# Splitting MLA queries and keys where the projections write them, and masking the score maxima on VectorE

## The chip, the cores and the metric

The kernel runs on one core of one Trainium2 chip. Its engines work side by side, each through its own queue in order: TensorE (PE in the profile, with its weight loads as PEld), VectorE (DVE), ScalarE (ACT), GpSimd (POOL) and SyncE (SP), which here issues most of the DMA transfers. The metric is the time of one execution on the device in microseconds, lower is better; the kernel before takes 2153.65 us, the median of three executions.

## What is computed

A decoder trunk of two layers over 1024 positions of width 1024. Layer 0 mixes positions by multi-head latent attention (MLA), layer 1 by a sliding window; each has four heads that look at a memory, an output projection and an MLP with squared ReLU. The change touches layer 0's MLA only. In the reference, cut to what matters:

```python
def mla_mixer(hn, positions, w_in, q_norm_g, kv_norm_g, w_uq, w_ukv):
    b, s, _ = hn.shape
    proj = hn @ w_in
    c_q, c_kv, k_r, q_cross = ...            # 384, 256, 32 and 256 columns
    q = (rmsnorm(c_q, q_norm_g) @ w_uq).reshape(b, s, 12, 96)
    q = jnp.concatenate([q[..., :64], rope(q[..., 64:], positions)], axis=-1)
    kv = (rmsnorm(c_kv, kv_norm_g) @ w_ukv).reshape(b, s, 12, 128)
    k_nope, v = kv[..., :64], kv[..., 64:]
    k_rope = jnp.broadcast_to(rope(k_r[:, :, None, :], positions), (b, s, 12, 32))
    k = jnp.concatenate([k_nope, k_rope], axis=-1)
    o = causal_dense_attention(q, k, v)      # softmax of q k / sqrt(96), k at or before q
    return o.reshape(b, s, 768), q_cross
```

There are 12 heads; a query or key has 64 columns of its own (nope) and 32 rotated ones (rope), and the rotated key is the same for all heads.

## The kernel before

A product in the kernel's precision is three matmuls. An operand `a` is split into a head `ah`, rounded to the TensorE format fp32r, and a rest `al = a - ah` (`split`, L96: ScalarE copies and rounds, L99; VectorE subtracts, L100; with a scale the same on L102 and L103). The matmuls are `ah bh`, `ah bl` and `al bh` (`mm3`, L108 to L110).

**Projection stage** (182 to 245 us of the span). `cTh` and `cTl` hold the split latent input, transposed. For each pair j of heads (6 of them) the nope keys come from TensorE into a PSUM tile `pskn` of 1024 positions and are copied whole in f32 to `kn[j]`, half by VectorE (L765) and half by ScalarE (L766). Then the rotary queries, eight position tiles t of 128: `q_rope(t)` multiplies (`psqr`) and rotates (`rope`, four VectorE products L302 to L305, two GpSimd sums L306 and L307, into a row tile `qt` in the quad tile `fa`); `q_ropeT(t)` transposes it on TensorE (`psqt`, L793) and ScalarE copies it to `qr` (L794, L795; two thirds of it lie in the tile `kq`). Between them `load_cols` brings the weights of the nope queries, nine pieces `wr` through two buffers (L533), and splits them into `wqn` and `wqn2`. `q_nope(j, i)` then makes the nope queries of pair j, half i of the positions (`psqn`), and copies them to `qn[j]` by ScalarE (i = 0, L777) or VectorE (L775).

**Head tiles.** `head_tiles(h)` collects the 96 rows of one head into staging tiles `q32` and `k32` by four DMAs (L710 to L713), and splits them into `qh`, `ql`, `kh`, `kl` (12 heads, tiles of 96 x 1024, in three sets `bufs_`). Row 96 of these tiles holds a row of ones (in the keys, L703) and the row's maximum (in the queries, L732 and L733), so that the scores come out with the maximum taken off. Set 0 has its own place; sets 1 and 2 lie in a pool `hb1` that takes the place of `cTh` and the weights after the projection stage.

**Head loop** (245 to 472 us). For head h the program runs `row_max` ahead: for each of eight query tiles i the scores of all keys up to the tile (`psx`, one matmul of heads only per 512 columns, L743), then a matmul of an identity with a mask that adds -1e30 above the diagonal (L744), then VectorE's maximum (L745). Rows with i > 3 use the one PSUM buffer "x", of two banks; those with i up to 3 share six buffers of one bank with all else. `max_row` transposes and splits the maxima. Then come the score blocks `scores(h, G, k)` (`pss`, three matmuls L865; a mask add on VectorE for diagonal blocks, L873; exponent on ScalarE, L875) and `values` (`pso`, L895). The score blocks of one head, its values and the maxima of a later head are interleaved. The values of head h are split by `v_tiles(h)` for all eight key tiles (`vh`, `vl`); key tiles 0 to 3 of the first half of the queries use the split, all blocks of the second half use unsplit values `vf`.

The order on each engine is that of the program after a scheduler has placed it; DMA issues stand in SP's queue in order, and one that waits holds those behind it.

Of the kernel before, what the change touches and what calls it, by code (L numbers as in the profile page):

```python
# [19 lines left out]
P = 128  # L20
D = 1024
S = 1024
# [33 lines left out]
def trunk(  # L56
# [450 lines left out]
    masks(pm)  # L507
# [197 lines left out]

    def head_tiles(h):
        r = slice((h % 2) * 64, (h % 2) * 64 + 64)
        q32 = hb.tile([96, S], F32, tag="q32", bufs=1, name=f"q32_{h}")
        k32 = hb.tile([96, S], F32, tag="k32", bufs=1, name=f"k32_{h}")
        nc.sync.dma_start(out=q32[0:64], in_=qn[h // 2][r, :])  # L710
        nc.sync.dma_start(out=q32[64:96], in_=qr[h // 4][(h % 4) * 32 : (h % 4) * 32 + 32, :])
        nc.sync.dma_start(out=k32[0:64], in_=kn[h // 2][r, :])
        nc.sync.dma_start(out=k32[64:96], in_=krs)  # L713
# [21 lines left out]
    def row_max(h, i):  # L735
# [5 lines left out]
        for a in range(0, n, 512):  # L741
            b = min(a + 512, n)
            nc.tensor.matmul(ps[:, a:b], qh[0:96, i * P : (i + 1) * P], kh[0:96, a:b], start=True, stop=b < n, skip_group_check=True)  # L743
        nc.tensor.matmul(ps[:, n - P : n], identb, dmask, start=False, stop=True, skip_group_check=True)  # L744
# [7 lines left out]
    krs = raw_tile([32, S], "krs")  # L752
# [3 lines left out]
    nc.vector.tensor_copy(krs, krT)  # L756
    for j in range(6):
# [7 lines left out]
        nc.vector.tensor_copy(kn[j][:, 0:512], ps[:, 0:512])  # L765
        nc.scalar.activation(kn[j][:, 512:1024], ps[:, 512:1024], AF.Copy)  # L766
# [1271 lines left out]
```

## Time and profile before

| | us |
|---|---|
| three executions | 2151.32, 2153.65, 2155.61 |
| median | 2153.65 |
| the profiled execution, time | 2155.25 |
| its span | 2153.2 |
| projection stage, 182 to 245 | 63 |
| head loop, 245 to 472 | 227 |

The span runs from the first to the last instruction on the chip; what lies around it is launch and end. All rows that the prediction quotes are of this one profiled execution. In a timeline row the first number is the start, the second the duration, both in us, then engine, line and operation, output and inputs by the program's names, shapes, and in brackets how long the engine stood idle before it and what released it. In a group row the last parts are the number of instructions, their busy time in us with the mean of one in ns, and the idle time ahead of them.

### The profile page before, as it was taken

Reading aid. Unit: us, or ns where it says so; the run is one execution under the profiler, and the core shown is the slowest. Engines: PE = TensorE matmul, PEld = TensorE weight load, DVE = VectorE, ACT = ScalarE, POOL = GpSimd, SP = SyncE. Lnnn points to the kernel's source line nnn. Section 1 sums busy time; section 2 is a strip of 40 time slices with the busy share of each in tenths; the row PEclk is TensorE's granted clock in tenths of the full one; section 3 lists DMA queues with packets and bytes.
Section 4 is the critical chain, followed back from the end, with each engine's and each line's share of the span. In section 5 each row is a group of like instructions: output and inputs, shape, how many; then the busy total and the mean of one; then the engine's idle time right before and its main releaser. Section 6 shows DMA issues by size and latency. Waiting matters only on the chain.

```text
span 2153.2 us, 29008 instructions
## 1 busy us (share of the span) xinstructions
PE 2121.7 (99%) x9877; PEld 1703.6 (79%) x9877; DVE 1468.2 (68%) x2905; ACT 1100.4 (51%) x2398; POOL 135.1 (6%) x223
## 2 busy tenths in 40 slices
PE   7999999999999999999999999999999999999998
PEld 6988766668887788888888878668888888888886
DVE  7566677764987677786657632775987776876565
ACT  5554465655754444444445432866754443444453
POOL 0001000000000000000001122530000000000000
PEclk9999999999999999999999999999999999999999
DMA  7102221333254445964543534142354446954442
GB/s 251 58 1 75 52 63 39 97 104 108 87 182 133 162 154 178 330 188 135 156 117 108 147 88 119 34 130 83 100 182 144 134 160 200 332 166 150 124 118 88
DMA packets 178498, 284.00 MB, mean 132 GB/s; under 512 B 17209, under 2 KB 73262, under 8 KB 178350
## 3 DMA queue, kind: packets, MB, share of 16 engines
q1 hardware_dynamic: 171908, 266.39, 40.0%
q0 software_dynamic: 4016, 13.12, 1.7%
q10 hardware_dynamic: 2426, 2.65, 0.4%
q8 instruction: 77, 1.26, 0.3%
q14 instruction: 71, 0.58, 0.1%
HBM read 180.13 MB, written 76.81 MB: 119 GB/s over the span
## 4 chain that ended last, share of the span: by engine, by line
PE 88%; DVE 5%; DMA 3%; ACT 2%; issue 1%; SPq 0%; POOL 0%; DVEq 0%; ACTq 0%
PE psy L1665 5%; PE psy L1667 5%; PE psy L1666 5%; PE psu L1362 5%; PE psu L1364 5%; PE psu L1363 5%; PE psz L1665 4%; PE psz L1666 4%; PE psz L1667 4%; PE psv L1362 4%; PE pso L895 4%; PE psv L1363 4%; PE psv L1364 4%; PE pss L865 3%; PE pswo L108 2%; PE pswo L109 2%
## 5 line engine op out<-in xcount | busy, mean ns | idle before, releaser
L1262 ACT ACTIVATE mr<-mr,gcol 128x256 f32<-128x256 f32 (+1 forms) x160 | 67.7, 480 | 79.2 <-DMA mr<-in_mlp_w_up_dram 75.4
L875 ACT ACTIVATE p<-pss 128x512 f32<-128x512 f32 (+2 forms) x144 | 68.6, 487 | 71.9 <-DVE pss L873 53.8
L1665 PE MATMUL psy<-g 128*128 128x512 f32 x256 | 99.9, 390 | 0.0
L1666 PE MATMUL psy<-g 128*128 128x512 f32 x256 | 99.6, 389 | 0.0
L1667 PE MATMUL psy<-g 128*128 128x512 f32 x256 | 99.4, 390 | 0.0
L99 ACT ACTIVATE g<-i 128x512 fp32r<-128x512 f32 x79 | 49.8, 631 | 92.8 <-PE psz L1666 45.9
L1262 ACT ACTIVATE d<-d,gcol 128x256 f32<-128x256 f32 x128 | 57.9, 503 | 71.2 <-DMA d<-in_mlp_w_up_dram 67.8
L100 DVE TENSOR_TENSOR g<-i,g 128x512 fp32r<-128x512 f32 x79 | 55.4, 701 | 48.9 <-ACT g L99 48.9
L99 ACT ACTIVATE i<-mr 128x512 fp32r<-128x512 f32 x78 | 49.3, 632 | 74.5 <-PE psy L1666 24.5
L745 DVE TENSOR_REDUCE m<-psx 128x1 f32<-128x768 f32 (+7 forms) x96 | 71.7, 752 | 22.1 <-PE psx L744 22.0
L99 ACT ACTIVATE uh<-i 128x512 fp32r<-128x512 f32 x66 | 41.8, 633 | 86.5 <-PE psy L1666 39.7
L895 PE MATMUL pso<-p,vf 128*128 128x512 f32 (+2 forms) x192 | 85.3, 528 | 0.0
L100 DVE TENSOR_TENSOR uh<-i,uh 128x512 fp32r<-128x512 f32 x66 | 45.6, 690 | 48.4 <-ACT uh L99 48.4
L1665 PE MATMUL psz<-g 128*128 128x512 f32 x192 | 74.7, 389 | 0.0
L1666 PE MATMUL psz<-g 128*128 128x512 f32 x192 | 74.7, 389 | 0.0
L1667 PE MATMUL psz<-g 128*128 128x512 f32 x192 | 74.7, 389 | 0.0
L100 DVE TENSOR_TENSOR i<-mr,i 128x512 fp32r<-128x512 f32 x78 | 53.6, 687 | 21.8 <-ACT i L99 21.8
L865 PE MATMUL pss<-qh,kh 97*128 97x512 f32 (+2 forms) x144 | 66.1, 464 | 0.1
L865 PE MATMUL pss<-ql,kh 97*128 97x512 f32 (+2 forms) x144 | 57.6, 400 | 0.0
L1578 DVE TENSOR_TENSOR mqf<-mqq,mqf 128x512 f32<-128x512 f32 x64 | 43.4, 688 | 19.3 <-DMA mqq<-in_mlp_w_down_dram 19.1
L1667 PEld LDWEIGHTS psy<-g 128*128 128x128 f32 x256 | 48.0, 188 | 10.0
L1665 PEld LDWEIGHTS psy<-g 128*128 128x128 f32 x256 | 48.1, 188 | 9.9
(645 smaller groups left out, 6861.6 us busy)
## 6 DMA issues: line engine op xcount, KB each, us to landing
i<-hd SPq DMA_DIRECT2D x154, 256.0 KB
hd<-uh SPq DMA_DIRECT2D x76, 256.0 KB
hd<-ul SPq DMA_DIRECT2D x76, 256.0 KB
mr<-in_mlp_w_up_dram SPq DMA_DIRECT2D x36, 512.0 KB
hd<-x SPq DMA_DIRECT2D x72, 256.0 KB
mr<-hd SPq DMA_DIRECT2D x70, 256.0 KB
d<-in_mlp_w_up_dram SPq DMA_DIRECT2D x32, 512.0 KB
mqq<-in_mlp_w_down_dram SPq DMA_DIRECT2D x32, 512.0 KB
```

What stands on the lines that cost most here:

```text
L99: nc.scalar.activation(hi, src, AF.Copy)
L100: nc.vector.tensor_tensor(lo, src, f32(hi), ALU.subtract)
L745: nc.vector.reduce_max(m8s[h][:, i : i + 1], ps[:, :n], axis=AX, negate=True)
L865: return lambda: nc.tensor.matmul(o, a, b, skip_group_check=True, **kw)
L895: mms.append(lambda: nc.tensor.matmul(o, a, b, skip_group_check=True, **kw))
L1262: nc.scalar.activation(w[:, k, :], w[:, k, :], AF.Copy, scale=g_mlp[layer][:, k0 + k : k0 + k + 1])
L1362: nc.tensor.matmul(ps, wh[:, k, :], xh[:, k, :], start=p in (1, 2, 5) and k == 0, stop=False, skip_group_check=True)
L1363: nc.tensor.matmul(ps, wh[:, k, :], xl[:, k, :], start=False, stop=False, skip_group_check=True)
L1364: nc.tensor.matmul(ps, wl[:, k, :], xh[:, k, :], start=False, stop=k == 3, skip_group_check=True)
L1665: nc.tensor.matmul(ps, ah[:, j, :], bh, start=p in (1, 5, 2) and k == 0, stop=False, skip_group_check=True)
L1666: nc.tensor.matmul(ps, ah[:, j, :], bl, start=False, stop=False, skip_group_check=True)
L1667: nc.tensor.matmul(ps, al[:, j, :], bh, start=False, stop=k == NP - 1, skip_group_check=True)
```

## The change

The nope keys, the nope queries, the rotary queries and the rotary key are split as they leave PSUM. The heads go, rounded, to where the f32 values went; the rests go to tiles `lo` (they use the buffers of `q32` and `k32`, in turn) and from there to DRAM tiles `kl_d`, `ql_d` (6 x 512 KB each) and `qrl_d` (8 x 192 KB, from the row tile that the rotation used). The rotary key's rest sits beside its head in `krs`. `head_tiles` now issues eight DMAs that write `qh`, `kh`, `ql`, `kl` directly, and splits nothing. The mask of the maxima's rows is added by VectorE to PSUM ahead of the maximum; the row i = 4, of 640 columns, is written as 320 + 320 around a bank's edge. The splits of the values for key tiles 4 to 7, which no matmul reads, go. `q_nope(0, 0)` stands one place earlier, ahead of the transpose of tile 6. The masks are made by GpSimd alone.

```diff
-    identb, dmask = [const.tile([P, P], BF16, name=n) for n in ("identb", "dmask")]
-    dmaskT = const.tile([P, P], F32, name="dmaskT")
-
-    def masks(pl):
-
-        nc.vector.tensor_copy(identb, ident)
-        for dst, sgn in ((dmask, 1), (dmaskT, -1)):
-            m = pl.tile([P, P], F32, tag="mask", bufs=2, name=f"mask{sgn}")
+    dmask, dmaskT = [const.tile([P, P], F32, name=n) for n in ("dmask", "dmaskT")]
+
+    def masks():
+
+        for m, sgn in ((dmask, 1), (dmaskT, -1)):
             nc.gpsimd.memset(m, 0.0)
             nc.gpsimd.affine_select(out=m, in_=m, compare_op=ALU.is_ge, fill=NEG, base=0, pattern=[[-sgn, P]], channel_multiplier=sgn)
-            nc.vector.tensor_copy(dst, m)
...
+    kl_d, ql_d = [[dram.tile([P, S], F32, name=f"{n}ld{j}") for j in range(6)] for n in "kq"]
+    qrl_d = dram.tile([P, 3, S], F32, name="qrld")
+
     def head_tiles(h):
         r = slice((h % 2) * 64, (h % 2) * 64 + 64)
-        q32 = hb.tile([96, S], F32, tag="q32", bufs=1, name=f"q32_{h}")
-        k32 = hb.tile([96, S], F32, tag="k32", bufs=1, name=f"k32_{h}")
-        nc.sync.dma_start(out=q32[0:64], in_=qn[h // 2][r, :])
-        nc.sync.dma_start(out=q32[64:96], in_=qr[h // 4][(h % 4) * 32 : (h % 4) * 32 + 32, :])
-        nc.sync.dma_start(out=k32[0:64], in_=kn[h // 2][r, :])
-        nc.sync.dma_start(out=k32[64:96], in_=krs)
-        qh, ql, kh, kl = bufs_[h % 3]
+        rr = slice((h % 4) * 32, (h % 4) * 32 + 32)
+        qh, ql, kh, kl = [f32(t_) for t_ in bufs_[h % 3]]
         if h in (1, 2):
             head_ones(h)
-        split(q32, qh[0:96], ql[0:96])
-        split(k32, kh[0:96], kl[0:96])
+        for dst, src in (
+            (qh[0:64], qn[h // 2][r, :]), (qh[64:96], qr[h // 4][rr, :]),
+            (kh[0:64], kn[h // 2][r, :]), (kh[64:96], krs[0:32]),
+            (ql[0:64], ql_d[h // 2][r, :]), (ql[64:96], qrl_d[rr, h // 4, :]),
+            (kl[0:64], kl_d[h // 2][r, :]), (kl[64:96], krs[32:64]),
+        ):
+            nc.sync.dma_start(out=dst, in_=src)
+
+    lo_ct = [0]
+
+    def lo_tile():
+        lo_ct[0] += 1
+        return hb.tile([P, S], F32R, tag=("q32", "k32")[lo_ct[0] % 2], bufs=1, name=f"lo{lo_ct[0]}")
+
+    def fr(ap):
+        return ap.bitcast(F32R)
...
@@ -738,10 +746,13 @@
         qh, ql, kh, kl = bufs_[h % 3]
         n = (i + 1) * P
         ps = psx(f"psx{h}_{i}") if i > 3 or len(psum) == 1 else ps1(f"psx{h}_{i}")
-        for a in range(0, n, 512):
-            b = min(a + 512, n)
-            nc.tensor.matmul(ps[:, a:b], qh[0:96, i * P : (i + 1) * P], kh[0:96, a:b], start=True, stop=b < n, skip_group_check=True)
-        nc.tensor.matmul(ps[:, n - P : n], identb, dmask, start=False, stop=True, skip_group_check=True)
+        if i == 4:
+            ps = ps[:, 192:832]
+        cut = 320 if i == 4 else 512
+        for a in range(0, n, cut):
+            b = min(a + cut, n)
+            nc.tensor.matmul(ps[:, a:b], qh[0:96, i * P : (i + 1) * P], kh[0:96, a:b], start=True, stop=True, skip_group_check=True)
+        nc.vector.tensor_tensor(ps[:, n - P : n], ps[:, n - P : n], dmask, ALU.add)
         nc.vector.reduce_max(m8s[h][:, i : i + 1], ps[:, :n], axis=AX, negate=True)
...
     qr = [kq[1][:, 2, :], kq[1][:, 3, :], raw_tile([P, S], "qr2")]
-    krs = raw_tile([32, S], "krs")
+    krs = raw_tile([64, S], "krs")
-    nc.vector.tensor_copy(krs, krT)
+    split(krT, fr(krs[0:32]), fr(krs[32:64]))
...
@@ -762,8 +773,10 @@
         ps = ps2(f"pskn{j}")
         mm3w([ps[:, s] for s in halves],
              [(wkn[kt][0][:, j * P : (j + 1) * P], wkn[kt][1][:, j * P : (j + 1) * P], [(cTh[:, 3 + kt, s], cTl[:, 3 + kt, s]) for s in halves]) for kt in range(2)])
-        nc.vector.tensor_copy(kn[j][:, 0:512], ps[:, 0:512])
-        nc.scalar.activation(kn[j][:, 512:1024], ps[:, 512:1024], AF.Copy)
+        lo = lo_tile()
+        for s in halves:
+            split(ps[:, s], fr(kn[j][:, s]), lo[:, s])
+        nc.sync.dma_start(out=kl_d[j], in_=f32(lo))
...
     def q_nope(j, i):
         ps = ps1(f"psqn{j}_{i}")
         mm3(ps, [(wqn[kt][0][:, j * P : (j + 1) * P], wqn[kt][1][:, j * P : (j + 1) * P], cTh[:, kt, halves[i]], cTl[:, kt, halves[i]]) for kt in range(3)])
+        if i == 0:
+            qlo[j] = lo_tile()
+        split(ps, fr(qn[j][:, halves[i]]), qlo[j][:, halves[i]])
         if i:
-            nc.vector.tensor_copy(qn[j][:, halves[i]], ps)
-        else:
-            nc.scalar.activation(qn[j][:, halves[i]], ps, AF.Copy)
-
-    qts = {}
+            nc.sync.dma_start(out=ql_d[j], in_=f32(qlo.pop(j)))
+
+    qts, qlo = {}, {}
...
@@ -791,8 +805,12 @@
         pt = ps1(f"psqt{t}")[:, 0:384]
         for i in range(3):
             nc.tensor.transpose(pt[:, i * P : (i + 1) * P], qt[:, i * P : (i + 1) * P], ident)
-        nc.scalar.activation(kq[1][:, 2:4, sl], pt[:, 0 : 2 * P].rearrange("p (k c) -> p k c", k=2), AF.Copy)
-        nc.scalar.activation(qr[2][:, sl], pt[:, 2 * P : 3 * P], AF.Copy)
+
+        lo = fr(qt).rearrange("p (k c) -> p k c", k=3)
+        p3 = pt.rearrange("p (k c) -> p k c", k=3)
+        split(p3[:, 0:2, :], fr(kq[1][:, 2:4, sl]), lo[:, 0:2, :])
+        split(p3[:, 2, :], fr(qr[2][:, sl]), lo[:, 2, :])
+        nc.sync.dma_start(out=qrl_d[:, :, sl], in_=f32(lo))
 
     for t in range(NT):
         q_rope(t)
@@ -800,8 +818,8 @@
             next(loading, None)
         if t > 1:
             q_ropeT(t - 2)
+    q_nope(0, 0)
     q_ropeT(NT - 2)
-    q_nope(0, 0)
     q_nope(0, 1)
     q_ropeT(NT - 1)
...
     for i in range(2):
-        vb = (at.tile([P, NT, 128], F32R, name=f"vh{i}"), at.tile([P, NT, 64], F32R, name=f"vl{i}"))
...
     def v_tiles(h):
         vh, vl = vbufs[h % 2]
-        src = v[:, :, h * 64 : (h + 1) * 64]
```

Three places show what moves. The first is SP's queue in the rotary part of the projection stage; `wr` is a piece of the query weights, the last figures of its name its place among nine. Before:

```order
L533 DMA wr_0_1_1_2109<-in_mla_w_uq_dram 128x384
L533 DMA wr_0_1_2_2137<-in_mla_w_uq_dram 128x384
L533 DMA wr_0_2_0_2165<-in_mla_w_uq_dram 128x384
L533 DMA wr_0_2_1_2193<-in_mla_w_uq_dram 128x384
L533 DMA wr_0_2_2_2221<-in_mla_w_uq_dram 128x384
L711 DMA q_0_2289<-kq_1891 32x1024
```

After (`qrld` is the DRAM tile of rotary rests, `fa` the tile it is stored from):

```order
L529 DMA wr_0_1_1_2141<-in_mla_w_uq_dram 128x384
L529 DMA wr_0_1_2_2172<-in_mla_w_uq_dram 128x384
L813 DMA qrld<-fa_98 384x1x128
L529 DMA wr_0_2_0_2203<-in_mla_w_uq_dram 128x384
L813 DMA qrld<-fa_98 384x1x128
L529 DMA wr_0_2_1_2234<-in_mla_w_uq_dram 128x384
L813 DMA qrld<-fa_98 384x1x128
L529 DMA wr_0_2_2_2265<-in_mla_w_uq_dram 128x384
L813 DMA qrld<-fa_98 384x1x128 x3
```

Between the weight loads now stand stores that each wait for a split; the order of the loads is as before.

The second is SP's queue at the end of the projection stage, where head 1's tiles (`kh_2466`, `kl_2467` before, `qh_2542` to `kl_2545` after) come into use. Before:

```order
L710 DMA q_1_2491<-qn_1889 64x1024
L711 DMA q_1_2491<-kq_1891 32x1024
L732 DMA qh_1897<-mhl_2404 1x8x128
L733 DMA ql_1898<-mhl_2404 1x8x128
L703 DMA kh_2466<-kh_1899 1x16x64
L703 DMA kl_2467<-kl_1900 1x16x64
L710 DMA q_2_2565<-qn_1889 64x1024
```

After (`qld_1894` is the last of the six DRAM tiles of query rests, `lo_2515` what it is stored from):

```order
L791 DMA qld_1893<-lo_2489 128x1024
L699 DMA kh_2544<-kh_1906 1x16x64
L791 DMA qld_1894<-lo_2515 128x1024
L699 DMA kl_2545<-kl_1907 1x16x64
L717 DMA qh_2542<-qn_1896 64x1024
L717 DMA qh_2542<-kq_1898 32x1024
L717 DMA kh_2544<-kq_1897 64x1024
L717 DMA kh_2544<-krs 32x1024
L717 DMA ql_2543<-qld_1889 64x1024
L717 DMA ql_2543<-qrld 32x1024
L717 DMA kl_2545<-kld_1883 64x1024
```

Head 1's loads, which stood ahead of the maxima of head 0 and went to staging tiles, now stand behind the ones rows of its own tiles, with the last store of query rests between them.

The third is TensorE's queue just after the projection stage: score blocks of head 0 (`pss`) and maxima's rows of head 1 (`psx`). Before:

```order
L865 MATMUL pss_1_4_2520<-qh_1897,kh_1899 128x512
L865 MATMUL pss_1_4_2520<-ql_1898,kh_1899 128x512
L865 MATMUL pss_1_4_2520<-qh_1897,kl_1900 128x512
L743 MATMUL psx_7_2528<-kh_2466,qh_2464 128x512 x2
L744 LDWEIGHTS identb
L744 MATMUL psx_7_2528<-dmask,identb 128x128
L865 MATMUL pss_0_1_2533<-qh_1897,kh_1899 128x384
L865 MATMUL pss_0_1_2533<-ql_1898,kh_1899 128x384
L865 MATMUL pss_0_1_2533<-qh_1897,kl_1900 128x384
```

After:

```order
L883 MATMUL pss_1_4_2596<-qh_1904,kh_1906 128x512
L883 MATMUL pss_1_4_2596<-ql_1905,kh_1906 128x512
L883 MATMUL pss_1_4_2596<-qh_1904,kl_1907 128x512
L883 MATMUL pss_0_1_2609<-qh_1904,kh_1906 128x384
L883 MATMUL pss_0_1_2609<-ql_1905,kh_1906 128x384
L883 MATMUL pss_0_1_2609<-qh_1904,kl_1907 128x384
L754 MATMUL psx_7_2604<-kh_2544,qh_2542 128x512 x2
L754 MATMUL psx_3_2621<-kh_2544,qh_2542 128x512
```

The mask matmul and the load of its identity are gone, and the first row of head 1 (`psx_7`) stands one score block later than before.

More of the change, by code (lines that the diff above doesn't have):

```diff
@@ L506, in trunk @@
     rope_tables(pm)
-    masks(pm)
+    masks()
     kv_d = [dram.tile([P, n], F32, name=f"kvd{i}") for i, n in enumerate((1024, 1024, 512))]
@@ L826, in trunk @@
     for i in range(2):
-        vb = (at.tile([P, NT, 128], F32R, name=f"vh{i}"), at.tile([P, NT, 64], F32R, name=f"vl{i}"))
+        vb = (at.tile([P, 4, 128], F32R, name=f"vh{i}"), at.tile([P, 4, 64], F32R, name=f"vl{i}"))
         vbufs.append(vb)
@@ L834, in v_tiles @@
         vh, vl = vbufs[h % 2]
-        src = v[:, :, h * 64 : (h + 1) * 64]
+        src = v[:, 0:4, h * 64 : (h + 1) * 64]
         if h < 2:
```

## The prediction

> **What bounds the kernel now.** I read the engine totals first, then busy time by stage in the windows view, then the timeline of the stages that the diff touches. The first row is the page's; the others give for each stretch its length and what each engine worked in it, the granted clock and the share of the DMA engines.
>
> ```profile
> PE 2121.7 (99%) x9877; PEld 1703.6 (79%) x9877; DVE 1468.2 (68%) x2905; ACT 1100.4 (51%) x2398; POOL 135.1 (6%) x223
> ...
> 182.00:197.60 15.60, 15.60 (x71) 12.88 (x70) 7.20 (x14) 6.64 (x14) 0.00 (x0) 1.00 0.49 145
> 197.60:212.10 14.50, 14.50 (x91) 14.26 (x89) 12.31 (x35) 5.89 (x16) 8.15 (x13) 1.00 0.40 109
> 212.10:221.00 8.90, 6.63 (x27) 5.21 (x25) 2.33 (x8) 2.93 (x9) 1.92 (x3) 0.81 0.00 1
> 221.00:245.00 24.00, 24.00 (x114) 18.85 (x113) 10.47 (x15) 4.93 (x10) 0.65 (x2) 1.00 0.15 34
> 245.00:262.80 17.80, 16.61 (x84) 11.63 (x83) 17.07 (x31) 11.88 (x23) 1.28 (x3) 1.00 0.35 82
> 297.70:315.20 17.50, 17.50 (x87) 12.29 (x87) 12.74 (x25) 11.25 (x23) 0.00 (x0) 1.00 0.28 61
> ```
>
> TensorE is busy 99% of the span, and all of 297.70 to 315.20, one period of the attention's head loop (17.5 us), where VectorE works 12.74 us. So a head gets shorter only by what leaves TensorE, and anything given to VectorE there is free while its answer is not waited for. Of the stretches shown it idles in two: 212.10 to 221.00 (2.27 us, before the query projection's second half) and 245.00 to 262.80 (1.19 us, heads 0 and 1 just after it, where VectorE works 17.07 of 17.80). The change touches both.
>
> **Masks leave TensorE.** 96 mask matmuls go. The rows are the group of those matmuls, VectorE's mask add of the score blocks, and score-maximum rows in the timeline.
>
> ```profile
> L744 PE MATMUL psx<-dmask,identb 128*128 128x128 bf16 x96 | 22.2, 231 | 0.0
> L873 DVE TENSOR_TENSOR pss<-pss,dmaskT 128x128 f32<-128x128 f32 x96 | 27.6, 292 | 14.1 <-PE pss L865 13.5
> ...
> 328.36 0.68 PE L743 MATMUL psx<-kh,qh 96*128 96x512 f32 x2
> 328.89 0.23 PE L744 MATMUL psx<-dmask,identb 128*128 128x128 bf16 x1
> 328.93 0.31 PE L865 MATMUL pss<-qh,kh 97*128 97x128 f32 x1
> 329.16 1.23 DVE L745 TENSOR_REDUCE m<-psx 128x1 f32<-128x1024 f32 x1 [0.29 <-PE psx L744]
> 329.71 0.39 PE L865 MATMUL pss<-qh,kh 97*128 97x512 f32 x1
> 329.94 0.40 PE L865 MATMUL pss<-ql,kh 97*128 97x512 f32 x1
> 330.18 0.40 PE L865 MATMUL pss<-qh,kl 97*128 97x512 f32 x1
> 330.43 0.30 PEld L743 LDWEIGHTS psx<-kh,qh 96*128 96x128 f32 x2 [0.30 <-DVE m L745]
> 331.22 1.09 DVE L745 TENSOR_REDUCE m<-psx 128x1 f32<-128x896 f32 x1 [0.43 <-PE psx L744]
> 333.48 0.51 PE L743 MATMUL psx<-kh,qh 96*128 96x512 f32 x2
> ```
>
> A row's 231 ns is not its price, since matmuls overlap. Starts are: 512 columns come every 0.235 us (329.71, 329.94, 330.18). From 328.36 to 328.93 two of them and the mask take 0.57 us, so the mask takes 0.57 - 0.47 = 0.10 here. Read from the mask's start alone (328.89 to 328.93) it would be 0.04; that is the lower bound, 96 x 0.04 = 3.8 us, and 0.231 x 96 = 22.2 us the upper. I take 0.12, the subtraction and a little for the weights that the mask loads between, since the stage is made of such spacings: **-11.5 us**. The Trainium skill, "TensorE: Matmul & The Clock Gate", section "Back-to-back issue gap", gives a sustained 81 ns for a 128-column matmul with its weight load; by it the term would be 7.8 us, and the sum 3.7 us worse. The one place quoted, 0.10, lies between the two.
>
> In exchange VectorE does 96 adds like L873's (0.292 us). They lie ahead of the reduce on the same PSUM slot, and the rows of over 512 columns have one slot. The row at 330.43 is that cost: the weights of the next such row wait for the reduce until 330.43, while TensorE's spacing (330.18 to 330.43) shows no loss yet: no slack. Afterwards the work between is 0.12 shorter and the reduce ends about 0.29 - 0.12 = 0.17 later, so this one row of a head gives its 0.12 back and pays 0.17: 0.30 us. The next row of the slot has slack: its reduce ends at 331.22 + 1.09 = 332.31, and the one after starts at 333.48, 1.2 us later. It and its like pay nothing. Seven heads of the steady loop have it: 2.1 us; heads 1 and 2, where VectorE is fuller, I set at 0.7. Bounds are 0 (VectorE, relieved below, answers earlier) and 96 x 0.30 = 29 us (every row waits). Taken, by the row with no slack: **+2.8 us**.
>
> **Splits leave the head loop.** Per head two ScalarE copies and two VectorE subtractions go, and half of one values split on each.
>
> ```profile
> L100 DVE TENSOR_TENSOR ql<-q,qh 96x1024 fp32r<-96x1024 f32 x12 | 14.6, 1216 | 3.5 <-ACT qh L99 3.5
> L100 DVE TENSOR_TENSOR kl<-k,kh 96x1024 fp32r<-96x1024 f32 x12 | 14.6, 1214 | 0.4 <-ACT kh L99 0.3
> ...
> 257.23 0.56 PE L743 MATMUL psx<-kh,qh 96*128 96x512 f32 x2 [0.43 <-DVE m L745]
> 259.48 0.33 PE L743 MATMUL psx<-kh,qh 96*128 96x128 f32 x1 [0.43 <-ACT p L875]
> ```
>
> VectorE loses 1.22 + 1.21 = 2.43 us and gains 8 x 0.29 = 2.3 us a head: nothing on balance, so it does not become the bound. But lumps of 1.2 us become pieces of 0.3, and waits like the two of 0.43 us in head 1 are such lumps. I credit those two and about 0.6 us more, **-1.5 us** (0 to -3). In steady heads the eight loads of a head, 1.57 MB in place of 0.79, are issued a head ahead and are needed some 9 us later; at the 262 GB/s of the slice quoted below they take 6 us. Hidden, on a cover of 3 us.
>
> **Head 1 now waits for its loads.** Its four tiles lie where the projection's input lay, which is free only after the last projection matmul at 244.75. Before, the loads went into staging tiles far earlier, and only the splits had to wait for that point. Now the loads themselves do.
>
> ```profile
> 222.23 0.58 SPq L710 DMA_DIRECT2D q<-qn  x1
> 225.25 1.06 ACT L99 ACTIVATE qh<-q 96x1024 fp32r<-96x1024 f32 x1 [1.34 <-DMA q<-qn]
> ...
> L765 DVE COPY kq<-pskn x6: 683/692/692, 184.2 to 197.8; 128x512 f32<-128x512 f32 x6
> ...
> 243.19 0.60 ACT L777 ACTIVATE fa<-psqn 128x512 f32<-128x512 f32 x1 [3.49 <-PE psqn L110]
> ...
> 244.75 0.40 PE L110 MATMUL psqn<-cTh,wqn2l 128*128 128x512 f32 x1
> 244.98 0.57 SPq L703 DMA_DIRECT2D kh<-kh  x1
> 247.53 0.73 PE L743 MATMUL psx<-kh,qh 96*128 96x512 f32 x2 [0.33 <-ACT kh L99]
> ...
> 248.03 0.52 SPq L710 DMA_DIRECT2D q<-qn  x1
> 249.87 0.60 SPq L713 DMA_DIRECT2D k<-krs  x1
> ...
> 251.00:252.00 1.00, 1.00 (x5) 0.56 (x4) 0.98 (x2) 0.93 (x2) 0.00 (x0) 1.00 1.00 262
> ```
>
> Count from 244.98. TensorE has three score blocks of head 0, which end at 247.53 - 0.33 = 247.2, now a fourth moved ahead (three times 384 columns, some 0.5 us), and then stands at head 1's first row (247.53, which waited 0.33 before). The queue of SP, in order: the ones row (0.57), the last store of query rests, which needs ScalarE's and VectorE's split of the last projection block (0.60 and 0.69 us for such a block, by its rows, after its end and some signalling: until about +1.7), the second ones row, then four loads of 0.5 to 0.6 each: the last is issued by about +4.3. A load that size takes 225.25 - 222.23 = 3.0 us from issue to use (the four issues from 248.03 to 249.87 show that spacing, and their data still fill the DMA engines from 251 to 252). So head 1's row starts near +7.3, and TensorE idles from 247.7 to about 252.2: 4.5 us, 4.2 more than before. A wait of that kind has a second price, seen after the 2.27 us idle at 212:
>
> ```profile
> 214.58 0.79 PE L793 MATMUL psqt<-ident,fa 128*128 128x128 f32 x3 [2.27 <-POOL fa L307]
> 215.60 0.63 PE L109 MATMUL psqn<-cTl,wqnh 128*128 128x512 f32 x1
> 216.03 0.63 PE L110 MATMUL psqn<-cTh,wqnl 128*128 128x512 f32 x1
> ...
> 208.55 0.33 SPq L533 DMA_DIRECT2D wr<-in_mla_w_uq_dram  x1
> 212.56 0.51 ACT L102 ACTIVATE wqn2h<-wr,gcol 128x256 fp32r<-128x256 f32 x1 [2.88 <-DMA wr<-in_mla_w_uq_dram]
> ```
>
> 512 columns come every 0.43 us there (215.60, 216.03) in place of 0.235, and the stretch's clock is 0.81: 0.19 x 8.90 = 1.7 us lost. The same page of the Trainium skill, in "What's actually happening", wants one idle window of about 3.4 us, free-running, before the clock drops; by it a 4.5 us idle has a whole window in it about a third of the time, an estimate of 0.6 us instead of 1.7. The 2.27 us idle that sufficed here speaks against the rule's letter. Together 4.2 + 1.7 = **+5.9 us**; bounds +2.2 (2.5 us idle, full clock) and +8 (6.6 us idle and the clock).
>
> **Splits enter the projection stage.** VectorE gets per position tile two subtractions (256 and 128 columns, by L873's 0.292 us for 128 about 0.42 + 0.29), six tiles of them in 197.60 to 212.10: 12.31 + 6 x 0.71 = 16.6 us in a stretch of 14.50, so it grows by 2.1. The weights of the query projection are loaded through two slots, each freed by VectorE; before, the last load was issued at 208.55 and split 4.0 us later, which is the 2.27 us idle. Later splits make later loads, and stores of rests (192 KB each) now stand in SP's queue between those loads. The first projection block now stands ahead of the transpose of 214.58, but needs the same last weights. The DMA engines fill too: by share they work 0.49 x 15.60 + 0.40 x 14.50 = 13.4 of the 30.1 us from 182.00 to 212.10; six stores of key rests (3.1 MB) and eight of rotary rests (1.6 MB) at 262 GB/s, the rate of the full slice above, add 18, which leaves no slack for the last weight loads. **+4 us** (2.1 for VectorE, 1.9 for half of a later 4.0 us load); bounds -0.5 (the gap swallows it all) and +10. In 221 to 245 VectorE has 10.47 of 24.00 and ScalarE 4.93: the six subtractions of 0.69 that come there hide, and the six more in 182.00 to 197.60 do (7.20 + 4.1 of 15.60). Three copies that built masks at the start go from VectorE, where TensorE does not wait for them: 0 to -0.9, taken as nothing.
>
> **Sum**: -11.5 + 2.8 - 1.5 + 5.9 + 4 = -0.3 us. The profiled execution took 2155.25 us (2.05 beside its span), 1.6 over the median 2153.65; the sum gives 2155.0 by its own time, and 2153.4 against the median, which I predict.
>
> **Rivals.**
> 1. *Both new waits are mostly hidden.* For it: TensorE already idles 2.27 us at the one place, and SP's queue may reach head 1's loads sooner. Head 1 costs 2.2 and the projection 0: -0.3 - 3.7 - 4 = -8.0, 2145.7 us.
> 2. *Slower: the projection's last weight loads stop overlapping.* In SP's queue each of the last two stands behind a store that waits for a split; from the point where that split is later than the slot's release, two round trips of 4.0 us follow one another. With 2.1 for VectorE +10.1 instead of +4: +5.8, 2159.5 us. For it: VectorE is 85% busy there (12.31 of 14.50), and the DMA engines would be full (above). Against: the stores may trail behind the loads, and from 212.10 on the DMA engines are idle.
> 3. *The masks are nearly free on TensorE*, 0.04 us each: the term is 3.8, the sum +7.4, 2161.1 us. Against it: the subtraction above.
> 4. *The mask add holds the slot in every row*, not one per head. Against it: the slack of 1.2 us; I give it no chance of its own.
>
> **How the numbers follow.** 0.2% is 4.3 us, about what a measurement here can tell from no change. The forecast, with its own range from -4.5 to +4, has 0.43; rival 1 0.25; rival 2 0.26; rival 3 0.04; others 0.02. Faster takes most of rival 1 and the forecast's edge, 0.26; slower most of rivals 2 and 3 and the other edge, 0.29; the same keeps 0.45. The range runs from 2145.0 to 2161.0, the middle of rival 1 less 0.7 and of rival 2 plus 1.5 us, which leaves 2 in 10 out.
>
> **What would show it.** Right: the steady head period falls from 17.5 to about 16.8 us, and the next wide row of each head waits some 0.3 us for a reduce; head 1's first row idles 4 to 5 us on a DMA, with clock near 0.5 after it; the query projection's second block starts 3 to 5 us later, after its idle. Wrong: a head period of 17.2 (masks cheap), no DMA wait at head 1, VectorE waits in every row, or a projection stage that ends over 6 us late.

## The result and the profile after

The changed kernel takes 2178.93 us (median of 4 executions, 2175.02 to 2181.25) where the one before takes 2153.80 (2151.32 to 2155.61): a ratio of 1.0116, 95% interval 1.0097 to 1.0134, some 25 us slower. The prediction said 2153.4, and its range ended at 2161.0.

The first rows are the windows view of both kernels, from 180 us to the first product of the output projection (465.6 us before, 491.1 after): length, busy time of TensorE, its weight loads, VectorE, ScalarE and GpSimd, then the granted clock, the DMA share and GB/s. First before, then after with four of its stages.

```profile
180.00:465.60 285.60, 280.67 (x1329) 199.53 (x1327) 193.78 (x381) 158.06 (x322) 13.22 (x22) 0.99 0.29 73
```

```profile
180.00:491.10 311.10, 288.56 (x1233) 206.01 (x1231) 203.10 (x481) 138.87 (x310) 11.76 (x22) 0.93 0.45 122
...
197.60:212.10 14.50, 13.41 (x75) 12.01 (x74) 11.56 (x34) 6.59 (x17) 5.63 (x10) 1.00 0.59 200
...
251.10:273.00 21.90, 16.24 (x66) 12.12 (x65) 14.16 (x33) 7.99 (x19) 1.84 (x5) 0.77 0.63 168
273.00:293.00 20.00, 16.03 (x57) 10.87 (x58) 11.94 (x28) 7.31 (x16) 0.00 (x0) 0.83 0.38 93
...
330.75:348.08 17.33, 16.89 (x77) 12.17 (x78) 12.35 (x33) 8.88 (x20) 0.00 (x0) 1.00 0.43 108
```

The stage is 25.5 us longer, which is the whole loss. TensorE idles 311.10 - 288.56 = 22.5 us in it in place of 4.9, so 17.6 us are waits. Its busy time rose by 7.9 us though 96 matmuls left it, and the clock column says why: 0.93 in place of 0.99, and the same matmuls take longer. The waits view (engine, line, releaser, total, times, longest) names the idle:

```profile
PE psx L754 <- DVE m L756: 6.9, 12, 1.6
PE psx L754 <- DMA kh<-krs: 5.6, 1, 5.6
PE psxt L733 <- DVE m L756: 2.9, 1, 2.9
...
PE psrc L980 <- DMA rTq<-rch: 1.7, 1, 1.7
PE psqr L108 <- DVE rb L301: 1.6, 2, 0.9
PE psqn L108 <- DVE rb L301: 1.3, 1, 1.3
```

The clock is read in windows of 3.41 us, here where the products that normalise finished heads (`psrc`) stand:

```profile
389.00:392.41 3.41, 1.72 (x7) 0.95 (x6) 1.36 (x3) 1.19 (x2) 0.00 (x0) 1.00 0.20 47
392.41:395.82 3.41, 3.41 (x8) 1.56 (x7) 0.57 (x2) 1.23 (x2) 0.00 (x0) 0.50 0.98 268
395.82:399.24 3.42, 3.42 (x7) 1.68 (x7) 2.79 (x7) 0.60 (x1) 0.00 (x0) 0.50 1.00 222
399.24:402.65 3.41, 3.41 (x7) 1.50 (x6) 1.18 (x4) 1.01 (x2) 0.00 (x0) 0.50 0.08 17
402.65:406.06 3.41, 3.41 (x8) 2.14 (x8) 1.71 (x4) 0.00 (x0) 0.00 (x0) 0.50 0.02 5
406.06:409.48 3.42, 3.42 (x16) 2.02 (x14) 2.14 (x8) 1.29 (x3) 0.00 (x0) 1.00 0.00 0
```

After a window that is half idle (1.69 us of waiting) the clock is 0.50 for four windows in which TensorE is busy throughout. In the whole stage there are 12 such windows after, at 242.2 (1), 255.9 (3), 279.8 (2), 392.4 (4) and 474.3 (2), and 1 before. The first four drops follow a window with a wait in it. The last does not: TensorE is busy all through the window ahead of it, which holds products of the second group of finished heads.

```profile
470.93:474.34 3.41, 3.41 (x14) 1.98 (x15) 2.13 (x5) 1.27 (x4) 0.00 (x0) 1.00 0.78 220
474.34:477.75 3.41, 3.41 (x8) 1.25 (x7) 0.91 (x3) 1.17 (x2) 0.00 (x0) 0.50 0.32 117
```

That gives a ledger for every kernel of this study: idle time of the stage; lost clock, which is half of TensorE's busy time in the windows at half clock; and work, busy time less lost clock. Against before (4.9, 1.7 and 279.0 us), each from one profiled execution. The last column is not from the profile: it is the granted clock over a whole execution, the mean of all executions of the row, and 0.001 of it is 2.2 us.

| kernel | median us | stage | idle | lost clock | work | windows at half clock | clock |
|---|---|---|---|---|---|---|---|
| before | 2153.8 | 0 | 0 | 0 | 0 | 1 | 0.9982 |
| changed | 2178.9 | +25.5 | +17.6 | +15.8 | -7.9 | 12 | 0.9908 |
| a masks alone | 2161.3 | +1.2 | +5.5 | +4.6 | -8.9 | 4 | 0.9948 |
| b early splits alone | 2182.3 | +25.0 | +10.2 | +16.2 | -1.4 | 11 | 0.9892 |
| c head 1's loads first | 2177.0 | +19.3 | +14.2 | +14.2 | -9.1 | 10 | 0.9920 |
| d normalising later | 2171.8 | +16.2 | +16.2 | +7.9 | -7.8 | 7 | 0.9938 |
| g three mends | 2164.5 | +11.6 | +11.6 | +8.2 | -8.2 | 6 | 0.9952 |
| k mends, low rows | 2162.0 | +3.2 | +5.0 | +2.8 | -4.7 | 3 | 0.9952 |
| f before, low rows | 2154.2 | -4.1 | +0.1 | 0.0 | -4.1 | 1 | 0.9975 |
| j before, mixed | 2149.5 | -6.9 | +0.2 | -1.7 | -5.4 | 0 | 0.9988 |
| m before, late head 1 | 2163.4 | +5.2 | +4.7 | +1.6 | -1.1 | 3 | 0.9962 |
| n before, late reciprocals | 2155.5 | +9.7 | 0.0 | +10.2 | -0.6 | 7 | 0.9978 |
| o before, half the values | 2153.5 | -3.3 | -0.3 | -1.7 | -1.3 | 0 | 0.9986 |

The lost clock is not a matter of one execution: 0.9908 against 0.9982 (the executions of before timed beside runs a to d; 0.9978 and 0.9983 beside the others) is 16 us. Two cautions on the use of the other columns. What follows the stage took from 1686 to 1693 us in these executions, so a median differs from before by a few us more or less than the stage does. And a single execution has windows at half clock or not by chance (run n).

Four places of the changed kernel make most of the idle. First, head 0's maxima in the projection stage: the timeline has VectorE's split of a projection block among the wide rows, and the transpose of the maxima waiting for the last of them. Most of this wait comes with the mask adds: with them alone (run a) the transpose waits 2.19 us, with the early splits alone (run b) it does not wait.

```profile
238.00 0.69 DVE L100 TENSOR_TENSOR lo<-psqn,qn 128x512 fp32r<-128x512 f32 x1 [0.29 <-ACT qn L99]
...
239.93 1.23 DVE L756 TENSOR_REDUCE m<-psx 128x1 f32<-128x1024 f32 x1
...
241.21 0.27 PE L733 MATMUL psxt<-ident,m 128*8 128x128 f32 x1 [2.86 <-DVE m L756]
```

Second, head 1's loads, as forecast: SP stands at the last store until 253.24, issues the fourth load at 256.11, and TensorE starts 3.5 us later.

```profile
253.24 0.32 SPq L791 DMA_DIRECT2D qld<-lo  x1
...
256.11 0.60 SPq L717 DMA_DIRECT2D kh<-krs  x1
...
259.62 1.62 PE L754 MATMUL psx<-kh,qh 96*128 96x512 f32 x3 [5.55 <-DMA kh<-krs]
```

Third, head 2's wide rows. They now stand almost one behind the other in TensorE's queue, and each waits for the mask add and the maximum of the one before, on the one PSUM buffer:

```profile
275.45 1.03 PE L754 MATMUL psx<-kh,qh 96*128 96x512 f32 x2
...
276.52 0.30 DVE L755 TENSOR_TENSOR psx<-psx,dmask 128x128 f32<-128x128 f32 x1 [0.41 <-PE psx L754]
...
276.86 1.22 DVE L756 TENSOR_REDUCE m<-psx 128x1 f32<-128x1024 f32 x1
...
278.23 0.64 PE L754 MATMUL psx<-kh,qh 96*128 96x512 f32 x2 [0.88 <-DVE m L756]
...
280.48 0.98 PE L754 MATMUL psx<-kh,qh 96*128 96x512 f32 x2 [1.61 <-DVE m L756]
...
282.94 0.87 PE L754 MATMUL psx<-kh,qh 96*128 96x320 f32 x2 [1.48 <-DVE m L756]
```

Fourth, the normalising products. They need the reciprocals of the denominators (`den`) of the first six heads, and these now come late by VectorE's order. Before, VectorE makes them 2.2 us after SP has issued the last store of the denominators, ahead of the wide rows that the normalising products follow on TensorE:

```profile
358.69 0.60 SPq L925 DMA_DIRECT2D den<-on  x1
360.86 0.94 DVE L945 RECIPROCAL rc<-den 48x128 f32<-48x128 f32 x1
...
364.07 1.23 DVE L745 TENSOR_REDUCE m<-psx 128x1 f32<-128x1024 f32 x1 [0.29 <-PE psx L744]
...
370.62 0.49 PE L962 MATMUL psrc<-rTq,sel 6*128 6x512 f32 x1
```

After, they stand behind three such rows, 10.9 us after the store, and VectorE has no idle time just ahead of them, so the store does not hold them:

```profile
376.86 0.64 SPq L943 DMA_DIRECT2D den<-on  x1
...
386.51 0.96 DVE L756 TENSOR_REDUCE m<-psx 128x1 f32<-128x768 f32 x1
...
387.72 0.94 DVE L963 RECIPROCAL rc<-den 48x128 f32<-48x128 f32 x1
...
389.06 0.81 SPq L968 DMA_DIRECT2D rTq<-rch  x1
...
391.52 0.50 PE L980 MATMUL psrc<-rTq,sel 6*128 6x512 f32 x1 [1.69 <-DMA rTq<-rch]
```

The order has changed so in run b too, with 1.15 us of wait, but not in run a: it comes with the early splits. Why the scheduler moved them is not shown.

A steady head, last, has the wait that the prediction drew: its second wide row waits for the add and the maximum.

```profile
330.75 0.64 PE L754 MATMUL psx<-kh,qh 96*128 96x512 f32 x2 [0.34 <-DVE m L756]
331.43 0.30 DVE L755 TENSOR_TENSOR psx<-psx,dmask 128x128 f32<-128x128 f32 x1 [0.42 <-PE psx L754]
```

But its period, 330.75 to the same row of the next head at 348.08, is 17.33 us. The prediction had about 16.8.

### The profile page after: what moved, and what is told of

It reads as the page before. It is cut to its first block, busy times and chain, and to the rows that moved or that the text cites. A ratio compares the mean times of both kernels' runs of the same rounds, so it can differ in the third digit from the quotient of the medians.

```text
span 2177.6 us, 29050 instructions
## 1 busy us (share of the span) xinstructions
PE 2128.2 (98%) x9781; PEld 1709.2 (78%) x9781; DVE 1479.3 (68%) x3002; ACT 1080.2 (50%) x2387; POOL 133.2 (6%) x223
## 4 chain that ended last, share of the span: by engine, by line
PE 90%; DVE 5%; DMA 2%; ACT 2%; issue 1%; SPq 0%; POOL 0%; ACTq 0%; DVEq 0%; POOLq 0%
PE psy L1683 5%; PE psu L1382 5%; PE psy L1685 5%; PE psu L1380 5%; PE psy L1684 5%; PE psu L1381 5%; PE psz L1683 4%; PE psz L1684 4%; PE psv L1382 4%; PE psv L1381 4%; PE psv L1380 4%; PE psz L1685 4%; PE pso L913 4%; PE pswo L110 2%; PE pss L883 2%; PE pswo L108 2%
## 5 line engine op out<-in xcount | busy, mean ns | idle before, releaser
L99 ACT ACTIVATE i<-mr 128x512 fp32r<-128x512 f32 x78 | 49.1, 629 | 79.4 <-PE psy L1684 25.5
L756 DVE TENSOR_REDUCE m<-psx 128x1 f32<-128x1024 f32 (+7 forms) x96 | 71.4, 753 | 1.6
L754 PE MATMUL psx<-kh,qh 96*128 96x384 f32 (+3 forms) x144 | 47.4, 387 | 12.5 <-DVE m L756 6.9
```

The source lines that it names most:

```text
L99: nc.scalar.activation(hi, src, AF.Copy)
L756: nc.vector.reduce_max(m8s[h][:, i : i + 1], ps[:, :n], axis=AX, negate=True)
```

## Experiments

The theory that the runs test, called clock theory in their expectations: new waits lose the time, each followed by windows at half clock. The rivals: VectorE's mask adds are the loss, or the splits in the projection stage are. All runs are timed against the kernel before on the same chip, whose medians there were 2154.2 (a to d), 2155.0 (f to k) and 2154.6 (m to o).

### a and b: each half of the change alone

Run a is the kernel before with this:

```diff
-        nc.tensor.matmul(ps[:, n - P : n], identb, dmask, start=False, stop=True, skip_group_check=True)
+        nc.vector.tensor_tensor(ps[:, n - P : n], ps[:, n - P : n], dmask, ALU.add)
```

(and the row of 640 columns as 320 + 320). Run b is the changed kernel with the reverse of it.

> The kernel before with the maxima's masks added by VectorE and nothing else of the change. Clock theory (the change loses by new waits, each followed by windows at half clock): no DMA wait at head 1, none ahead of the first normalisation product, one slot wait of about 0.3 us per steady head, 0 to 2 windows at half clock beyond the two of before; 2150 to 2158 us. Rival 1 (VectorE's mask adds in the row's slot are the loss): the 0.3 us waits and those of heads 0 to 2 stay as in the changed kernel, 2168 us or more. Rival 2 (the splits in the projection stage are the loss, the masks gain what was forecast): 2143 to 2147 us.

> The changed kernel with the mask matmuls back on TensorE: early splits alone. Clock theory: the waits at head 1 (about 5.5 us) and ahead of the first normalisation product (1.7 us) stay, with 7 windows at half clock after them; the row waits go; 2165 to 2176 us. Rival 1 (mask adds are the loss): within 4 us of before. Rival 2 (the splits are the loss): slower than the changed kernel, 2183 us or more.

Run a took 2161.31 us, ratio 1.0034 (1.0021 to 1.0047); run b 2182.33 us, 1.0124 (1.0106 to 1.0141). So the early splits alone cost as much as the whole change, and the first rival falls. But the second does not follow: in b the work on TensorE is 1.4 us less than before, and its loss is idle time (+10.2) and clock (+16.2). Neither result lies in the theory's range: b is 6 us above it, and a 3 us above it, between it and the first rival's. Of the 11 windows at half clock of b, 6 (at 392.9 and 471.4) follow a window in which TensorE was busy throughout. The steady heads of a gain (the transposes of two neighbouring heads stand at 328.95 and 345.59, a period of 16.64 us where the kernel before has 17.47) and have no wait like the 0.34 us above: two value products that stand behind that row in the changed kernel stand ahead of it here. These places give the gain back:

```profile
235.67 0.27 PE L721 MATMUL psxt<-ident,m 128*8 128x128 f32 x1 [2.19 <-DVE m L744]
...
258.97 0.90 PE L742 MATMUL psx<-kh,qh 96*128 96x320 f32 x3 [1.16 <-DVE m L744]
271.63 0.58 PE L742 MATMUL psx<-kh,qh 96*128 96x512 f32 x2 [1.11 <-DVE m L744]
```

The stage of a ends only 1.2 us late; the other 6 us of its median lie behind the stage. Set product by product against the kernel before, the profiled execution loses them mostly in six steps of 0.7 to 1.7 us between 514 and 1843 us, where the program is the same; their cause is open.

### c and d: one wait mended at a time

Run c, on the changed kernel: the four loads of heads (of head 1, and of head 2 likewise) are issued ahead of the ones rows, and GpSimd issues the last store of query rests. Its second part is:

```diff
-            nc.sync.dma_start(out=ql_d[j], in_=f32(qlo.pop(j)))
+            (nc.gpsimd if j == 5 else nc.sync).dma_start(out=ql_d[j], in_=f32(qlo.pop(j)))
```

Run d, on the changed kernel, moves the normalising products of every group of heads:

```diff
-            if n == GRP[c + 1] * NB + LB + 6:
+            if n == GRP[c + 1] * NB + LB + 10:
                 muls = rc_mul(c)
```

> The changed kernel with head 1's four loads of heads ahead of its ones rows, and the last store of query rests issued by GpSimd, so that SP does not hold them. Clock theory: TensorE's wait at head 1's first row falls from 5.6 to about 2.5 us and the half clock there from three windows to one or two: 5 to 7 us off, 2172 to 2174 us. Idle alone counts: 3 us off, 2176 us. If the loads are late for another reason: no change.

> The changed kernel with the products that normalise finished heads (psrc) four steps later in each group. Clock theory: the 1.7 us wait on the transposed reciprocals goes, and with it the four windows at half clock after 392 us: 6 to 9 us off, 2170 to 2173 us. Idle alone counts: 1.7 us off, 2177 us. If thin work and not the wait holds the clock down: the half clock stays though the wait goes, 2175 to 2179 us.

Run c took 2177.00 us, 1.0100 (1.0084 to 1.0115). The wait at head 1 fell from 5.55 to 2.82 us and the half clock behind it from three windows to one, and the stage ends 6.2 us sooner, as the theory has it; of that 1.9 us reach the median, which lies outside the theory's range and 1 us above what idle alone gives. By the time alone it does not speak for the theory. Run d took 2171.84 us, 1.0076 (1.0059 to 1.0094): 7.1 us for a wait of 1.7 us, in the theory's range. Idle time fell by 1.4 us and lost clock by 7.9. But only 3.4 of these 7.9 stand where the wait was: two windows at half clock remained at 402.8 us with no wait ahead of them, the third case of its expectation, in part. Another 3.4 are the two windows at 474.3, which no wait preceded and which this edit moved along with the products there, and 1.6 a window at head 1, which the edit does not touch. So run d shows that the place of these products matters for the clock, not that the wait does.

### m and n: one wait put into the kernel before

Run m puts the staging tiles of head 1 where its loads can start only when the projection has ended. Run n sends the reciprocals of the first six heads through two more DRAM tiles, by GpSimd's queue. Of each edit this is the main part:

```diff
+        if h == 1:
+            q32, k32 = [f32(bufs_[2][e])[0:96] for e in (0, 2)]
+        else:
...
+            if c == 0:
+                for q in range(2):
+                    d_ = dram.tile([6, S], F32, name=f"hop{e}{q}")
+                    nc.gpsimd.dma_start(out=d_, in_=src)
+                    src = d_
```

> The kernel before with one thing changed: the staging tiles of head 1 lie in head 2's tiles, in the memory that the projection's input leaves, so that head 1's loads can only start when the projection has ended, as in the changed kernel; then they are split as before. Clock theory: TensorE idles 6 to 8 us ahead of head 1's first row (loads about 5.5, then two copies of 1.05 us), and two or three windows at half clock follow, 1.7 us each for those not already idle: the attention stage ends 8 to 12 us later than before, 2162 to 2166 us. Idle alone: 6 to 8 us later, no half clock.

> The kernel before; the reciprocals of the first six heads take two detours through DRAM on GpSimd's queue on their way to the tile that the normalising products read, which had some 6 us to spare. Clock theory: if they come late, TensorE idles 1 to 4 us there and one to four windows at half clock follow: the attention stage ends 3 to 9 us later. Idle alone: later by the idle time only. If they are still in time: no change.

Run m took 2163.40 us, 1.0035 (1.0019 to 1.0050), as expected:

```profile
252.44 1.22 PE L746 MATMUL psx<-kh,qh 96*128 96x512 f32 x2 [7.16 <-ACT kh L99]
```

One wait, 6.8 us more than before, and three windows at half clock (248.8 to 259.0, in part idle), 3.3 us of lost clock. The profiled execution's stage ends 5.2 us late, less than the 8 to 12 expected: it was among the quicker ones, idle elsewhere was 2 us less, and the one window at half clock of the kernel before did not come. So a wait brings the clock down here.

Run n took 2155.53 us, 1.0006 (0.9997 to 1.0016): the reciprocals were in time, no change. But one of its 11 executions, the profiled one, took 2167.15 where the others lie between 2153.11 and 2159.55, and it shows what the theory did not have. These are TensorE's first normalising product and windows of 3.41 us from there:

```profile
371.62 0.50 PE L968 MATMUL psrc<-rTq,sel 6*128 6x512 f32 x1
```

```profile
372.00:375.41 3.41, 3.41 (x13) 2.08 (x13) 2.01 (x4) 1.23 (x2) 0.00 (x0) 0.99 0.02 3
375.41:378.82 3.41, 3.41 (x7) 1.07 (x5) 1.71 (x4) 0.79 (x2) 0.00 (x0) 0.50 0.00 0
...
392.48:395.89 3.41, 3.41 (x12) 2.61 (x11) 0.89 (x4) 0.53 (x2) 0.00 (x0) 0.51 0.83 216
395.89:399.30 3.41, 3.41 (x21) 2.96 (x21) 0.96 (x4) 2.74 (x6) 0.00 (x0) 1.00 0.00 0
```

Six windows at half clock, 10.2 us lost, and TensorE was busy all through and in the window ahead. So a wait can be enough for the clock to fall, but where the normalising products stand it also falls without one: here in one of 11 executions, and in the profiled executions of the changed kernel (474.3), b, c, d and g as well. What stands there are products of 6 or fewer rows (`6*128` in the row) between score and value blocks.

### o: the values' splits alone

```diff
-        src = v[:, :, h * 64 : (h + 1) * 64]
+        src = v[:, 0:4, h * 64 : (h + 1) * 64]
```

> The kernel before without the unread half of the values' splits (key tiles 4 to 7), which no matmul reads; nothing else. Both theories: VectorE and ScalarE lose about 0.25 us a head, off the path: within 1.5 us of before, 2152 to 2155 us. A gain of 3 us or more would mean that these lumps held the rows of the maxima.

2153.51 us, 0.9997 (0.9985 to 1.0010): no difference, as expected.

### f and j: masks on VectorE where they gain

Both start from the kernel before; `dve` picks the rows whose mask VectorE adds (from a bf16 tile), the others keep the matmul. Run f has the first condition; run j the second, and the edit of run o.

```diff
+        dve = i < 4
+        dve = i < 4 or 2 < h < 8
```

> The kernel before; only the maxima's rows with i up to 3, which share six PSUM buffers, get their mask from VectorE; rows with i over 3, on the one buffer, keep the mask matmul. Slot theory (a mask on VectorE gains what leaves TensorE except where the one buffer is held): half the masks leave TensorE and no row wait appears; the attention stage ends 3 to 5 us sooner than before, 2149 to 2152 us. Rival (VectorE's extra adds cost as such, in whatever row): no gain or a loss, 2154 us or more. Rival (the masks are nearly free on TensorE, 0.04 us): 2 us sooner, 2152 to 2154 us.

> As the run with the low rows, and all rows of heads 3 to 7 masked by VectorE, where those heads showed a period of 16.65 us with all masks on VectorE and no waits above 0.3 us; besides, the unread half of the values' splits dropped. Slot theory: 5 x 4 more masks off TensorE, 0.1 us each: 5 to 7 us sooner than before in the attention stage, 2147 to 2150 us. Rival (adds cost as such): slower than the run with the low rows alone.

Run f took 2154.16 us, 0.9994 (0.9985 to 1.0003). Its stage ends 4.1 us sooner, by work alone (-4.1 for 48 masks, no new wait), as the slot theory has it; but the median is above the 2149 to 2152 expected, and the gain is not in the time. In the profiled execution 1.6 us of it go to a second window at half clock just behind the stage (463.1 to 469.9; before has one there, at 467.3); where the rest went is open. Run j took 2149.45 us, 0.9978 (0.9969 to 0.9987), faster than both kernels and in its range; 1.7 of the 6.9 us of its stage are the one window at half clock of before, which did not come here. The rows are transposes of two neighbouring heads' maxima, a period of 16.85 us.

```profile
306.56 0.27 PE L725 MATMUL psxt<-ident,m 128*8 128x128 f32 x1
...
323.41 0.27 PE L725 MATMUL psxt<-ident,m 128*8 128x128 f32 x1
```

### g and k: how far the early splits can be mended

Run g has the edits of c and d, and takes head 0's maxima up one projection block later (`n == 8` for `n == 7` ahead of `max_row(0)`). Run k adds the condition of run f.

> The changed kernel with three mends together: head 1's loads of heads first, the normalising products four steps later, and the transpose of head 0's maxima one projection block later (so that TensorE does not wait 2.9 us for VectorE there). If each wait and its half-clock windows are worth what they cost singly: the attention stage ends 6 (first), 9 (second) and 4 (third) us sooner than in the changed kernel, near 472 us, 2158 to 2163 us. If waits only move to the next place: 2168 to 2172 us.

> The same three mends, and the mask matmuls back for the rows with i over 3 (those on the one PSUM buffer). Slot theory: the four waits of 0.9 to 1.6 us in a run at the start of head 2 get shorter by 0.2 to 0.3 us each, the 0.33 us wait of each steady head goes, the masks on TensorE cost 4 us: within 3 us of the run with the mends alone. Rival (mask adds are the loss): 8 us or more below that run.

Run g took 2164.53 us, 1.0043 (1.0029 to 1.0057): 14.4 us below the changed kernel, between the two ranges of its expectation and less than the sum of the three, since 3.2 us of waiting stayed at head 1, 1.3 at the transpose, and three windows at half clock near 396, with TensorE busy throughout the window ahead of them. Run k took 2161.98 us, 1.0044 (1.0028 to 1.0059), no different from g by time. Its stage is 8.4 us shorter, which is the rival's figure, so what the mask adds of the wide rows cost in the mended kernel is not settled.

## Why the prediction was wrong

The sum was -0.3 us; the stage shows +25.5. Two steps failed above all: the clock, charged at one window for one wait, and the waits of the first heads for VectorE's mask adds. Term by term:

**Masks leave TensorE, -11.5: right sign, too large.** The ledger's work column gives -7.9 for 96 masks in the changed kernel, -4.1 for 48 in run f, -5.4 for 68 (and half a values' split) in run j, -8.9 for 96 in run a: 0.08 to 0.09 us each, below both the 0.12 taken and the 0.10 read at one place, which the steady heads of run a come near (0.83 us for 8). The Trainium skill's 81 ns ("TensorE: Matmul & The Clock Gate", section "Back-to-back issue gap"), which the prediction set aside, is close to these.

**The mask add on the one buffer, +2.8: 8.8, wrong at the start.** The wait of 0.30 us per steady head came as 0.33, eight times. But head 2 alone waits 0.88 + 1.61 + 1.48 us, and head 0's row and transpose, put at nothing, 0.31 + 2.86; less the 1.0 us of such waits before, this is 8.8. Run b, which has the early splits and not the adds, has 2.6 us of such waits in place of the 9.8 here. The step that failed is "heads 1 and 2, where VectorE is fuller, I set at 0.7", a figure without a row. What decided was the order: head 2's wide rows stand one behind the other, with two value products after the first and nothing between the rest. Slack read from the old trace holds only while the same work stands between the rows. The same holds the other way: in the steady heads of run a the order changed and the wait did not come. The period that the text gave as the sign of being right, about 16.8 us, is that of run a (16.64); the changed kernel has 17.33, near the 17.2 that it gave as a sign of being wrong. Of the 0.7 us between the two kernels 0.34 is this wait; the rest was not placed.

**Splits leave the head loop, -1.5: not seen, as far as can be told.** The steady period of run b, with early splits and the masks on TensorE, was 17.44 us (17.47 before).

**Steady loads hidden: right for the loads; what else moves was not asked.** No row of a steady head waits for a load. But the reciprocals of the first six heads, which nothing in the sum prices, moved behind three wide rows in VectorE's queue, and their chain ends at TensorE with 1.7 us of wait.

**Head 1's wait: right in mechanism.** 4.5 us of idle were forecast, 5.55 came, by the queue that the text spelled out; run m shows such a wait alone.

**Projection stage, +4: about right for what it priced.** `q_nope`'s first product starts at 218.11 us, 3.1 later than 215.03 before. VectorE fell behind and TensorE waits for rotations in pieces (0.7 to 1.3 us). But the last projection product starts at 250.90 where it started at 244.75, 6.2 us late, past the 6 that the prediction named as a sign of being wrong: the other 3.2 us are the two waits of head 0's maxima, which stand in this stage. The weight loads of rival 2 were not the bound there, and the DMA engines, which the estimate had full, are at a share of 0.59 from 197.60 to 212.10.

**The clock, +1.7: the largest miss.** The prediction charged one window for one wait. There were 12 against 1: 17.5 us less the 1.7 of before, 15.8. Three waits of the first heads brought 6 windows, 7.3 us. The other 6, 10.2 us, stand at the normalising products: four after the wait of 1.7 us, two after none. No term of the sum has either these products or a clock that stays at half while TensorE is busy. The half clock of the kernel before lasts a single window, in the projection; carrying that length to the head loop was the error. Its trace has one more, just behind the stage, after a window in which TensorE was 85% busy:

```profile
463.90:467.31 3.41, 2.90 (x10) 1.13 (x9) 3.38 (x4) 2.17 (x5) 0.00 (x0) 1.00 0.53 179
467.31:470.72 3.41, 3.02 (x9) 2.57 (x10) 3.38 (x9) 2.80 (x7) 0.00 (x0) 0.50 0.81 277
```

Of the 25.5 us, idle time makes 17.6, lost clock 15.8, and the masks return 7.9. The idle time is the waits for maxima (8.8), head 1's loads (5.2), the projection stage's other waits (2.0) and the reciprocals (1.7). That the mask matmuls' absence helps the clock to fall was not tried; run b, which has them, lost as much.

Rival 2 had the slower side, by the wrong mechanism. Rival 4, given no chance, is what head 2 shows. No rival had several waits with their clock.

## What to carry to other kernels

Where a tuned loop keeps TensorE busy without a gap, a new wait costs its length and some clock behind it (17.6 us of idle came with 15.8 us of lost clock here, not all of it behind waits; in run m 6.8 us with 3.3). Count all waits: read the queue behind every DMA that is added, and the order of every engine after the change, for rows that share one buffer and now stand side by side and for small steps that now stand behind long ones. Work that moves off a full engine to one with time to spare pays only where nobody waits for the answer: 68 of the 96 masks, with the values' edit, gained 0.2% (run j), 48 of them changed nothing in the time (run f), all 96 lost 0.3% (run a). An early split saves nothing in TensorE's time (17.44 us a head in run b, 17.47 before) while the engines that did it late were never waited for.

## What the hardware showed

The granted clock is 0.50 or 1.00 over windows whose edges lie on one grid of 3.413 us through an execution: the drops at 242.2, 255.9, 279.8, 392.4 and 474.3 us are 4, 7, 33 and 24 windows apart. It fell after windows with 1.7 us of idle (392.4), but also with none, at 474.3 in the changed kernel and at 375.4 in run n, where it stayed at half for six windows. The Trainium skill, "TensorE: Matmul & The Clock Gate", section "What's actually happening", ties the drop to an idle window and the return to a busy one; the busy time in these rows does not decide either.

Products of 6 or fewer rows stand where it fell without idle time, which suggests that the use of the array counts and not the busy time. The traces bear this out for the drop. Take as use of a window the columns that the matmuls starting in it stream, each weighted with its share of the 128 x 128 array; a window of nothing but full products, 512 columns every 0.235 us, would have 7,400. Between 180 and 2130 us the 13 traces have 36 windows that a drop follows. Their use is at most 3,008, with TensorE busy at least 99% of the window in 7 of them; no drop follows any of the 7,241 windows with more. Low use does not always bring a drop: below 1,700 it came after 15 of 16 windows, from there to 3,010 after 21 of 100. What decides there, and when the clock returns, is open, and no run changes the use alone.
